# Seven block products in place of eight for the gate and up projections of layer 1

## The chip, the cores and the metric

The kernel runs on one core of a Trainium2 chip. The time is device microseconds (us) of one execution. In a span lie the instructions of five engines that run beside each other: TensorE (PE: matmuls; PEld: its weight loads), VectorE (DVE), ScalarE (ACT), GpSimd (POOL) and SyncE (SP, which here only issues DMAs). Each engine takes its instructions in the written order; semaphores make one wait for another. POOL also issues most DMAs.

## The reference, cut to what matters

640 tokens (512 latent, 128 context) of width 1024 pass through two layers. Each layer is feed-forward, mixer (layer 0 attention, layer 1 a long convolution named Hyena), feed-forward; so there are four feed-forwards, and the changed ones are the two of layer 1. One is

```
h = x * (1 + scale) + shift
g, u = split(h @ w1)            # w1: 1024 x 5632, so g and u: 640 x 2816
f = (silu(g) * u) @ w2          # w2: 2816 x 1024
x = layer_norm(ALPHA * x + 0.5 * gate * f)
```

`shift`, `scale` and `gate` come from `silu(cond) @ ada_w`, nine vectors of 1024 for each layer. The Hyena mixer needs the spectra of its filters, which depend on the weights alone.

## The kernel before, in words

Everything is held transposed: features on the 128 partitions, 640 tokens along the row, in two halves of 320. To keep accuracy each operand is split in a high part rounded to the multiplier's format (fp32r) and a low part, the remainder; one product then takes three matmuls: high by high, high by low, low by high.

The program runs in this order: spectra of the Hyena filters with the first modulation vectors (`spectra`), feed-forward 0 of layer 0, attention, feed-forward 1 of layer 0, feed-forward 0 of layer 1, Hyena, feed-forward 1 of layer 1. By the profile's times these begin at about 0, 169, 640, 940, 1417, 1888 and 2257 us.

- `ffn`: the 2816 hidden features are 22 chunks of 128 in four parts (`PARTS`, 6, 6, 6 and 4). For each chunk `ffn1` computes g and u (L561: 8 blocks of 128 inputs, 2 outputs, 3 matmuls, for each half: 96 matmuls of 320 columns), then ACT takes SiLU (L569), DVE multiplies (L571) and `split` makes the high part on ACT (L93) and the low part on DVE (L94). After each part the second product runs (`mm_cols`, L522): an output tile of 128 features and one half takes 18 matmuls, and `resid` (L503, DVE) adds it to x.
- Weights come in units. `w_dma` (L113, POOL) loads one, which gives the high part; `w_split` copies it negated on ACT (L125) and adds the raw weights to it by an accumulating DMA that POOL issues (L126), which leaves the low part. `w_get(i)` splits a unit ahead while fewer than `wmax` (3) are live. They share 8 buffers.
- `bg_step` makes one block of 128 values of a modulation vector beside the feed-forward: two DVE reductions (L255) over a 512 KB piece of `ada_w`, which POOL loaded two steps ahead into one of two buffers (L241). Before, the steps of layer 1's vectors lie in feed-forward 1 of layer 0 (60 places) and feed-forward 0 of layer 1.
- `spectra` is a software pipeline of rounds r. In a round PE generates filter block r+6 (`gen`) and transforms block r (`xform`, L1104); DVE multiplies with the decay (`decay`, L1019), combines (`comb`, L1070), makes low parts (`lo`, L1088) and takes the larger of two magnitudes (`total`, L1046); ACT makes high parts (`hi`, L1080, L1082), magnitudes (`mags`, L1029) and stores the transforms (`store`, L1119). Low parts of the second of two operands come by an accumulating DMA of 256 KB (L1087).

PSUM holds 8 tiles, taken in turn for every product.

Of the kernel before, what the change touches and what calls it, by code (L numbers as in the profile page):

```python
# [21 lines left out]
FF = 2816  # L22
NF = 22
PARTS = [(0, 6), (6, 12), (12, 18), (18, 22)]
ALPHA = 4.0 ** 0.25
EPS = 1e-5
TWO_PI = (6.28125, 0.0019340515136718750, 1.255665914356996e-06)
# [15 lines left out]
class Kernel:  # L43
# [492 lines left out]
    def group_steps(self, us, fn):  # L536
# [4 lines left out]
                out.append((u, (lambda w, u=u, half=half: fn(w, u, half)), half == 1))  # L541
        return out

    def ffn(self, l, f, u0):
        nc = self.nc
        u = u0
        i_ln = 0 if f == 0 else 2
        sums = {}

        def ffn1(c):  # L550
            def fn(w, u, half):
                self.flush(f"ln{half}")
                a, z = self.half[half]
                wh, wl = w
                g = self.ps(name="g")
                uu = self.ps(name="u")
                for k in range(KD):
                    xh, xl = self.h[k]
                    for o, c0 in ((g, 0), (uu, P)):
                        for q, (s, m) in enumerate(((wh, xh), (wh, xl), (wl, xh))):  # L560
                            nc.tensor.matmul(o[:, 0:z - a], s[:, k, c0:c0 + P], m[:, a:z],  # L561
                                             start=(k == 0 and q == 0), stop=(k == 7 and q == 2))
                    self.clk(6 * 0.136)
                ci = c - part[0]
                if ci not in acts:
                    acts[ci] = (self.b(dt=F32R, name="ah"), self.b(dt=F32R, name="al"))
                ah, al = acts[ci]
                sg = self.t((P, z - a), name="sg")
                nc.scalar.activation(out=sg, in_=g[:, 0:z - a], func=AF.Silu)  # L569
                ac = self.t((P, z - a), name="ac")  # L570
                nc.vector.tensor_tensor(out=ac, in0=sg, in1=uu[:, 0:z - a], op=ALU.mult)  # L571
                self.split(ah[:, a:z], al[:, a:z], ac)
            return fn

        for pi, part in enumerate(PARTS):
            acts = {}
            fin = pi == len(PARTS) - 1
            c = part[0]
            while c < part[1] - fin:
                n = 3 if c == 0 else 1  # L580
                self.run_steps(self.group_steps(range(u, u + n), lambda w, q, half, d=c - u: ffn1(q + d)(w, q, half)), c > 0)
                u += n
                c += n
            if pi == 0:
                self.flush("ln0x")
                self.flush("ln1x")
                gt = self.gate(l, 2 + 3 * (2 if f else 0), 0.5)
            ks = [(q, q) for q in range(part[1] - part[0])]
            if not fin:
                for jj in range(4):  # L590
                    w = self.w_get(u)
                    for j2 in range(2):
                        for half in range(2):
                            ps = self.ps(name="f")
                            self.mm_cols(ps, w, j2 * P, acts, ks, half)
                            self.resid(ps, jj * 2 + j2, half, gt)
                        self.bg_step()
                    self.w_done(u)
                    u += 1
            else:  # L600
                out = (l, f) == (1, 1)
                if out:
                    self.half, self.seg = HALF2, SEG2
                else:
                    GB = self.sh(l, i_ln)

                def fn(w, q, half, u=u, c=c):
                    if q == u:
                        ffn1(c)(w, q, half)
# [12 lines left out]
                self.run_steps(self.group_steps(range(u, u + 3), fn))  # L622
                u += 3
        return u
# [345 lines left out]
    def spectra(self):  # L970
# [18 lines left out]
        def w3_hi(n):  # L989
            w3[n] = [self.fp.tile([P, 512], F32R, tag="w3", name="w3", bufs=6) for _ in range(3)]  # L990
            nc.scalar.activation(out=w3[n][0], in_=self.xs(2), func=AF.Copy)
            nc.scalar.activation(out=w3[n][1], in_=self.xs(0), func=AF.Copy)

        def w3_lo(n):
            wa, wb, wl = w3[n]
            nc.vector.tensor_tensor(out=wl[0:64], in0=self.xs(2)[0:64], in1=wa[0:64].bitcast(F32), op=ALU.subtract)
            nc.vector.tensor_tensor(out=wl[64:P], in0=self.xs(0)[64:P], in1=wb[64:P].bitcast(F32), op=ALU.subtract)
            if n + 1 < 4:
                self.w3_load(n + 1)

# [131 lines left out]
        for r in range(-6, NI):  # L1132
# [4 lines left out]
            on(decay, r + 5)  # L1137

            ahead = [r + 2] if r < 14 else [16, 17] if r == 14 else [r + 3]
            middle = r % 5 == 1 and 0 <= r + 5 < NI  # L1140
            if middle:
                on(mags, r + 5)
                mid(r + 5)
            for i in ahead:
                on(comb, i)
                on(hi, i)
                on(lo, i)
            if not middle:
                on(mags, r + 5)
# [417 lines left out]
    def run(self):  # L1567
        nc, tc, I, O = self.nc, self.tc, self.I, self.O
        with ExitStack() as es:
# [36 lines left out]
            with tc.tile_pool(name="fq", bufs=1) as fq:  # L1606
                self.ada_pool(fq, 16 * KD)
                u = self.ffn(0, 1, u)
                u = self.ffn(1, 0, u)
                self.need_mods(1, range(9))  # L1610
            with tc.tile_pool(name="hp", bufs=1) as self.ap:
                u = self.hyena(u)
            u = self.ffn(1, 1, u)
            for h in range(2):
                self.flush(f"ln{h}")

    def add_ffn_units(self, units, l, f):
        I = self.I
        for pi, (p0, p1) in enumerate(PARTS):
            for c in range(p0, p1):  # L1620
                units.append((I["w1"][l, f, c], [P, KD, 256]))
# [8 lines left out]
def host_layout(i):  # L1630
# [148 lines left out]
```

## Time and profile before

| | us |
|---|---|
| median of 3 runs | 2754.49 (2753.18 to 2756.75) |
| profiled execution | 2754.99 |
| its span | 2753.2 |
| PE busy | 2657.8 (97%) |
| DVE, ACT, POOL busy | 1319.8, 890.2, 724.4 |
| mean granted TensorE clock | 0.988 of full |

Matmuls overlap, so their durations (about 310 ns) are longer than their distance. The distance comes from the chain of waits, where a run of matmuls stands as one piece. In a list of groups the last columns tell the busy time, the mean duration and the idle time of the engine before, with who ended it.

### The profile page before, as it was taken

The numbers are of one execution on the slowest core, as the hardware profiler recorded it, in microseconds if no ns is written. First come the engines' busy times: TensorE is split into PE (matmuls) and PEld (weight loads), VectorE is DVE, ScalarE is ACT, GpSimd is POOL, SyncE is SP. The second block draws the span as 40 slices with busy tenths as digits, with TensorE's granted clock in tenths as the row PEclk, the third lists the DMA queues.
The fourth block names the chain that finished last, engine by engine and source line by source line (L and its number), as shares of the span: only waits on it lengthen the run. The fifth ranks groups of instructions, "written<-read, shape, count | busy, mean of one in ns | idle before, by whom it ended". The sixth has DMA issues, their size and how long they took to land.

```text
span 2753.2 us, 42540 instructions
## 1 busy us (share of the span) xinstructions
PE 2657.8 (97%) x17402; PEld 2519.5 (92%) x17402; DVE 1319.8 (48%) x2894; ACT 890.2 (32%) x1518; POOL 724.4 (26%) x980
## 2 busy tenths in 40 slices
PE   8889999999899999999999999999999899999997
PEld 3679999998845899999999999999999899999997
DVE  6845555627864446555555311116439843211114
ACT  3662212125675332222242222124323333122222
POOL 3521121215122422121241111114119742101103
PEclk9999999999999999999999999999999999999998
DMA  7667978854302669797856856663653365656561
GB/s 244 195 194 200 283 216 242 233 156 106 95 16 61 169 155 254 202 264 208 256 131 178 215 141 154 145 165 95 181 168 130 109 180 131 164 129 176 129 163 54
DMA packets 91802, 460.22 MB, mean 167 GB/s; under 512 B 10975, under 2 KB 16687, under 8 KB 57560
## 3 DMA queue, kind: packets, MB, share of 16 engines
q0 software_dynamic: 71136, 405.50, 56.1%
q1 hardware_dynamic: 20104, 51.96, 5.5%
q8 instruction: 137, 2.24, 0.3%
q14 instruction: 57, 0.47, 0.1%
q10 hardware_dynamic: 368, 0.04, 0.0%
HBM read 436.22 MB, written 16.01 MB: 164 GB/s over the span
## 4 chain that ended last, share of the span: by engine, by line
PE 63%; issue 15%; DVE 6%; POOL 5%; DMA 2%; ACT 2%; SPq 0%; POOLq 0%; DVEq 0%; ACTq 0%
PE f L522 18%; PE g L561 17%; PE u L561 17%; PE u L522 6%; PE o L815 2%; POOL ar L241 1%; PE pt L804 1%; POOL wh L113 1%; DMA wl<-w 1%; DVE yl L1383 1%; DVE q L682 1%; POOL wl L126 1%; PE s L780 1%; DVE p L1354 1%; PE s L781 0%
## 5 line engine op out<-in xcount | busy, mean ns | idle before, releaser
L125 ACT ACTIVATE wl<-wh 128x2048 fp32r<-128x2048 f32 (+1 forms) x167 | 297.8, 1783 | 449.5 <-PE f L522 351.5
L561 PE MATMUL g<-hh,wl 128*128 128x320 f32 (+1 forms) x1408 | 435.8, 310 | 3.4 <-DMA wl<-w 3.4
L522 PE MATMUL f<-al,wh 128*128 128x320 f32 (+2 forms) x1408 | 436.5, 310 | 2.1 <-DVE al L94 1.6
L522 PE MATMUL f<-ah,wl 128*128 128x320 f32 (+2 forms) x1408 | 435.9, 310 | 1.7 <-DMA wl<-w2a 1.0
L522 PE MATMUL f<-ah,wh 128*128 128x320 f32 (+2 forms) x1408 | 437.3, 311 | 0.0
L561 PE MATMUL g<-hh,wh 128*128 128x320 f32 (+1 forms) x1408 | 437.3, 311 | 0.0
L561 PE MATMUL g<-hl,wh 128*128 128x320 f32 (+1 forms) x1408 | 435.7, 309 | 0.0
L561 PE MATMUL u<-hh,wl 128*128 128x320 f32 (+1 forms) x1408 | 435.5, 309 | 0.0
L561 PE MATMUL u<-hl,wh 128*128 128x320 f32 (+1 forms) x1408 | 435.5, 309 | 0.0
L561 PE MATMUL u<-hh,wh 128*128 128x320 f32 (+1 forms) x1408 | 435.5, 309 | 0.0
L571 DVE TENSOR_TENSOR ac<-sg,u 128x320 f32<-128x320 f32 (+1 forms) x176 | 85.8, 487 | 671.8 <-ACT sg L569 671.6
L503 DVE SCALAR_TENSOR_TENSOR x<-f,gate,x 128x128 f32<-128x128 f32 (+3 forms) x432 | 173.6, 435 | 314.7 <-PE f L522 314.2
L569 ACT ACTIVATE sg<-g 128x320 f32<-128x320 f32 (+1 forms) x176 | 76.9, 437 | 758.4 <-PE g L561 758.4
L522 PEld LDWEIGHTS f<-al,wh 128*128 128x128 f32 x1408 | 265.2, 188 | 3.9 <-DVE al L94 3.7
L561 PEld LDWEIGHTS g<-hh,wl 128*128 128x128 f32 x1408 | 264.7, 188 | 3.9 <-DMA wl<-w 3.9
L522 PEld LDWEIGHTS f<-ah,wl 128*128 128x128 f32 x1408 | 265.1, 188 | 2.2 <-DMA wl<-w2a 1.2
L522 PEld LDWEIGHTS f<-ah,wh 128*128 128x128 f32 x1408 | 265.1, 188 | 1.0 <-ACT ah L93 0.5
L561 PEld LDWEIGHTS g<-hl,wh 128*128 128x128 f32 x1408 | 264.6, 188 | 1.2 <-POOL hl L318 0.5
L561 PEld LDWEIGHTS g<-hh,wh 128*128 128x128 f32 x1408 | 264.7, 188 | 0.5
L561 PEld LDWEIGHTS u<-hl,wh 128*128 128x128 f32 x1408 | 264.8, 188 | 0.0
L561 PEld LDWEIGHTS u<-hh,wh 128*128 128x128 f32 x1408 | 264.7, 188 | 0.0
L561 PEld LDWEIGHTS u<-hh,wl 128*128 128x128 f32 x1408 | 264.7, 188 | 0.0
(315 smaller groups left out, 4685.5 us busy)
## 6 DMA issues: line engine op xcount, KB each, us to landing
wh<-w POOLq DMA_DIRECT2D x86, 1024.0 KB, 11.2
wl<-w POOLq DMA_DIRECT2D x86, 1024.0 KB, 9.1
ar<-ada_w POOLq DMA_DIRECT2D x128, 512.0 KB, 5.9
wh<-w2a POOLq DMA_DIRECT2D x48, 768.0 KB, 10.7
wl<-w2a POOLq DMA_DIRECT2D x48, 768.0 KB, 9.2
wh<-hyin POOLq DMA_DIRECT2D x12, 1024.0 KB, 10.8
wl<-hyin POOLq DMA_DIRECT2D x12, 1024.0 KB, 8.0
wr<-ada_first SPq DMA_DIRECT2D x8, 1024.0 KB
```

The source lines that it names most:

```text
L113: nc.gpsimd.dma_start(out=r, in_=src)
L125: self.nc.scalar.activation(out=lo, in_=hi.bitcast(F32), func=AF.Copy, scale=-1.0)
L126: self.nc.gpsimd.dma_start(out=lo, in_=self.units[i][0], accum_op=ALU.add)
L241: self.nc.gpsimd.dma_start(out=self.ada_raw[n], in_=self.I["ada_w"][l, m, j])
L503: nc.vector.scalar_tensor_tensor(out=self.x[:, j, s0:s1], in0=ps[:, s0 - a:s1 - a], scalar=gate[:, tk, j:j + 1], in1=self.x[:, j, s0:s1], ...
L522: nc.tensor.matmul(ps[:, 0:z - a], s[:, kw, c0:c0 + P], m[:, a:z], start=(first and i == 0 and q == 0), stop=(last and i == n - 1 and q == 2))
L561: nc.tensor.matmul(o[:, 0:z - a], s[:, k, c0:c0 + P], m[:, a:z], start=(k == 0 and q == 0), stop=(k == 7 and q == 2))
L569: nc.scalar.activation(out=sg, in_=g[:, 0:z - a], func=AF.Silu)
L571: nc.vector.tensor_tensor(out=ac, in0=sg, in1=uu[:, 0:z - a], op=ALU.mult)
L682: nc.vector.tensor_tensor(out=tiles[r][R[1 - r], c], in0=x[R[r]], in1=tiles[r][R[r], c].bitcast(F32), op=ALU.subtract)
L780: nc.tensor.matmul(ps[:, 0:n], x, kh[t][:, r, c0:c0 + n], start=True, stop=False)
L815: nc.tensor.matmul(ob[R[r], :], v[:, vs[c], g * 64:(g + 1) * 64], pts.pop((b, g, c)), start=(c == 0), stop=(c == len(vs) - 1))
```

## The change

1. Layer 1's feed-forwards take `ffn_s`. Chunks 0, 1, 2 and 21 are computed as before. For chunks 3 to 20 `s_unit` treats inputs in two halves (r), tokens in two halves of 320 and outputs as gate and up, and computes the 2x2 block product with seven products instead of eight (Winograd's form of Strassen's scheme). A product is 4 blocks of 128 inputs by 3 matmuls of 320 columns, 12 matmuls; a chunk is 84.
2. The sums of token blocks are made once for each feed-forward (`s_tokens`: POOL adds high and low parts again, DVE makes four sums, `split` parts them). The sums of weight blocks are made for every chunk one chunk ahead (`s_weights`, four pieces p0 to p3, called from `hooks` between the products): SP loads four blocks of 256 KB, POOL makes two sums, DVE two more, ACT and DVE split them, and the three plain blocks get their low part by an accumulating DMA.
3. The hidden features are seven parts of 3, 3, 3, 3, 3, 3 and 4 chunks (`PARTS7`). In the second product a tile takes 9 matmuls.
4. All modulation vectors of layer 1 are made in feed-forward 1 of layer 0: in the second products of its first two parts `bg_step` runs twice at each place (76 places for 72 steps).
5. In `spectra` magnitudes and their sum are of block r+4 and no longer r+5, so they follow the decay by a round; the low part of the filters' last weights comes by two accumulating DMAs after the first group.

```diff
+    def s_weights(self, c, nxt):
...
+        def block(n, g, r):
+            h, l = ops[n]
+            x = A.pop((c, g, r)) if n == "a22" else A[c, g, r]
+            nc.scalar.activation(out=h, in_=x, func=AF.Copy)
+            nc.scalar.activation(out=l, in_=x, func=AF.Copy, scale=-1.0)
+            nc.gpsimd.dma_start(out=l, in_=self.I["w1s"][self.sf, c, g, r], accum_op=ALU.add)
+
+        def p0():
...
+            block("a11", 0, 0)
+            nc.gpsimd.tensor_tensor(out=st["s"][:, 1], in0=A[c, 1, 0], in1=A[c, 1, 1], op=ALU.add)
+            block("a12", 0, 1)
...
+        def p1():
+            slot(("s2", "s3"))
+            nc.vector.tensor_tensor(out=st["d"], in0=st["s"][:, 1], in1=A[c, 0, 0], op=ALU.subtract)
+            nc.gpsimd.tensor_tensor(out=st["s"][:, 0], in0=A.pop((c, 0, 0)), in1=A.pop((c, 1, 0)), op=ALU.subtract)
+            self.split(*ops["s2"], st["d"])
+            self.split(*ops["s3"], st["s"][:, 0])
...
+        def p2():
+            slot(("a22", "s1"))
+            block("a22", 1, 1)
+            nc.vector.tensor_tensor(out=st["d"], in0=A.pop((c, 0, 1)), in1=st["d"], op=ALU.subtract)
+            self.split(*ops["s1"], st["s"][:, 1])
...
+        def p3():
+            slot(("s4",))
+            self.split(*ops["s4"], st["d"])
...
+    def s_unit(self, c, acts, ci, hooks):
...
+        x = prod("a11", B[0, 0])
+        nc.scalar.activation(out=s1, in_=x, func=AF.Copy)
+        hook(0)
+        x = prod("a12", B[1, 0])
+        add(sg, s1, x)
+        nc.scalar.activation(out=sg, in_=sg, func=AF.Silu)
+        hook(1)
+        x = prod("s2", Tn[2])
+        add(u2, s1, x)
+        hook(2)
+        x = prod("s3", Tn[3])
+        add(u3, u2, x)
+        hook(3)
+        x = prod("a22", Tn[4])
+        add(s1, u3, x)
+        nc.vector.tensor_tensor(out=s1, in0=sg, in1=s1, op=ALU.mult)
+        self.split(ah[:, n], al[:, n], s1)
+        hook(4)
+        x = prod("s1", Tn[1])
+        add(u2, u2, x)
+        add(u3, u3, x)
+        hook(5)
+        x = prod("s4", B[1, 1])
+        add(u2, u2, x)
+        nc.scalar.activation(out=u2, in_=u2, func=AF.Silu)
+        nc.vector.tensor_tensor(out=u3, in0=u2, in1=u3, op=ALU.mult)
+        self.split(ah[:, 320:T], al[:, 320:T], u3)
...
+                if i < 2:
+                    w = self.s_weights(c + 1, after[c + 1])
+                    hooks = {0: w[0], 1: w[1], 3: w[2], 5: w[3]}
+                if i == 1:
+                    def cast(m=u + 1):
+                        self.wlim = m
+                        self.w_dma(m)
+                    hooks[4] = cast
+                if i == 2:
+                    def cast(m=u + 2):
...
+                    hooks[0] = cast
+                    hooks[2] = self.w_split
+                self.s_unit(c, acts, i, hooks)
+            if not fin:
+                w = self.s_weights(c1, after[c1])
+                second(u, acts, gt, {1: w[0], 4: w[1], 7: w[2], 10: w[3]})
...
                         self.bg_step()
+                        if pi < 2 and f:
+                            self.bg_step()
...
-            if not middle:
-                on(mags, r + 5)
-            on(total, r + 5)
+            on(total, r + 4)
```

On ACT, in a feed-forward of layer 1, two halves of a chunk read before as SiLU (`sg`), high part of the activations (`ah`), and then the copy of a unit's weights (`wl`):

```order
L569 ACTIVATE sg_14891<-g_14839 128x320
L93 ACTIVATE ah_14889<-ac_14893 128x320
L569 ACTIVATE sg_14947<-g_14897 128x320
L93 ACTIVATE ah_14889<-ac_14949 128x320
L125 ACTIVATE wl_14953<-wh_14718 128x1536
```

Now it reads as below in the second chunk of a part and the beginning of the third. `sw` are the operands of the next chunk, made from the raw blocks `sr` or the sums `s13` and `s24`; `sa` are the activations, `sm` a product, `wl` the low part of the second product's first weights.

```order
L95 ACTIVATE sw_14296<-s13_14269 128x512
L619 ACTIVATE sw_14333<-sr_14192 128x512
L620 ACTIVATE sw_14333<-sr_14192 128x512
L95 ACTIVATE sw_14333<-s13_14269 128x512
L95 ACTIVATE sa_14253<-s1_14249 128x320
L95 ACTIVATE sw_14378<-s24_14270 128x512
L708 ACTIVATE u2_14250<-u2_14250 128x320
L95 ACTIVATE sa_14253<-u3_14251 128x320
L685 ACTIVATE s1_14399<-sm_14405 128x320
L689 ACTIVATE sg_14402<-sg_14402 128x320
L127 ACTIVATE wl_14450<-wh_14361 128x1536
```

The third chunk's first product (L685) stands behind the last activation of the second (L95 `sa`), and `wl` behind the third chunk's first SiLU.

On POOL, in feed-forward 1 of layer 0, the second product of the first part read before with two pieces of `ada_w` (`ar`) for each unit of weights:

```order
L126 DMA wl<-w2a 128x1536
L113 DMA wh<-w 128x2048
L241 DMA ar<-ada_w 128x1024 x2
L126 DMA wl<-w 128x2048
L113 DMA wh<-w 128x2048
```

and now, at the same place, with four:

```order
L128 DMA wl<-w2a 128x1536
L115 DMA wh<-w 128x2048
L243 DMA ar<-ada_w 128x1024 x4
L128 DMA wl<-w 128x2048
L115 DMA wh<-w 128x2048
```

A unit's accumulating DMA (`wl`) stands behind twice as many pieces, each of which waits for a step of DVE.

On ACT in `spectra`, a round read before with the high parts (`sh`, `sl`) ahead of the magnitudes (`am`) and the stores (`sg`):

```order
L1080 ACTIVATE sh<-cb 128x512 x2
L1082 ACTIVATE sl<-cb 128x512
L1029 ACTIVATE am<-ab 128x512 x2
L1119 ACTIVATE sg<-xf 128x2x256 x2
L1080 ACTIVATE sh<-cb 128x512 x2
```

Now the magnitudes stand first, and they are of the block whose decay was in the round before:

```order
L1281 ACTIVATE am<-ab 128x512 x2
L1332 ACTIVATE sh<-cb 128x512 x2
L1334 ACTIVATE sl<-cb 128x512
L1371 ACTIVATE sg<-xf 128x2x256 x2
L1281 ACTIVATE am<-ab 128x512 x2
```

In a round they have moved from behind `sl` to the front.

## Rows read from the trace of the kernel before

**Rows 1.** The page: busy time of each engine, its share, instructions.
```profile
PE 2657.8 (97%) x17402; PEld 2519.5 (92%) x17402; DVE 1319.8 (48%) x2894; ACT 890.2 (32%) x1518; POOL 724.4 (26%) x980
```
**Rows 2.** Windows: the engines' busy us (instructions), PE clock, DMA share, GB/s.
```profile
50.00:150.00 100.00, 82.80 (x333) 60.59 (x331) 78.41 (x108) 67.97 (x126) 53.46 (x54) 0.93 0.63 174
...
1033.00:1075.00 42.00, 42.00 (x288) 42.00 (x287) 28.21 (x55) 7.24 (x6) 9.58 (x15) 1.00 0.89 256
...
1547.00:1631.00 84.00, 84.00 (x575) 84.00 (x574) 11.46 (x24) 20.09 (x28) 8.53 (x12) 1.00 0.57 144
...
2347.00:2389.00 42.00, 42.00 (x289) 42.00 (x288) 10.20 (x25) 7.57 (x6) 5.69 (x8) 1.00 0.70 169
```
**Rows 3.** Chain of waits, 1550 to 1700 us: start, length, engine, line, matmuls.
```profile
1549.87 0.44 PE g L561 x3
...
1631.71 42.24 PE f L522 x288
```
**Rows 4.** Groups by line in feed-forwards: busy us, mean ns, idle before, who ended it.
```profile
L571 DVE TENSOR_TENSOR ac<-sg,u 128x320 f32<-128x320 f32 x174 | 84.8, 487 | 659.7 <-ACT sg L569 659.6
L94 DVE TENSOR_TENSOR al<-ac,ah 128x320 fp32r<-128x320 f32 x174 | 87.0, 500 | 93.6 <-ACT ah L93 93.6
L93 ACT ACTIVATE ah<-ac 128x320 fp32r<-128x320 f32 x174 | 82.1, 472 | 114.2 <-DVE ac L571 114.2
L569 ACT ACTIVATE sg<-g 128x320 f32<-128x320 f32 x174 | 76.0, 437 | 732.1 <-PE g L561 732.1
L125 ACT ACTIVATE wl<-wh 128x1536 fp32r<-128x1536 f32 x48 | 70.8, 1475 | 96.3 <-PE f L522 56.3 <-issue 40.0
L503 DVE SCALAR_TENSOR_TENSOR x<-f,gate,x 128x320 f32<-128x320 f32 x136 | 74.7, 549 | 154.6 <-PE f L522 154.3
```
**Rows 5.** Timeline of DVE, ACT and POOL, two stretches of `spectra`: start, length, what.
```profile
77.74 1.28 DVE L1070 TENSOR_TENSOR cb<-ab 128x512 f32<-128x512 f32 x2
79.12 0.69 DVE L1088 TENSOR_TENSOR sl<-cb,sh 128x512 fp32r<-128x512 f32 x1
81.28 0.69 DVE L1046 TENSOR_TENSOR am<-am 128x512 f32<-128x512 f32 x1 [1.47 <-ACT am L1029]
...
80.12 1.13 ACT L1029 ACTIVATE am<-ab 128x512 f32<-128x512 f32 x2
...
49.89 1.27 POOL L1050 TENSOR_TENSOR am<-am 128x512 f32<-128x512 f32 x1 [0.68 <-DVE am L1046]
51.12 1.71 POOL L1023 TENSOR_TENSOR ab<-ab 1x512 f32<-1x512 f32 x1
...
50.85 2.53 DVE L1070 TENSOR_TENSOR cb<-ab 128x512 f32<-128x512 f32 x2
```
**Rows 6.** Timeline of POOL, 1555 to 1610 us.
```profile
1606.34 0.87 POOL L126 DMA_DIRECT2D wl<-w2a  x1 [12.23 <-ACT wl L125]
1606.90 0.86 POOL L113 DMA_DIRECT2D wh<-w2a  x1
```
**Rows 7.** Landing times: issues of L126 at 1600 to 1780, 1560 to 1605 us; the page.
```profile
DMA to landing us min/median/max: 6.6/7.8/8.4
...
DMA to landing us min/median/max: 7.9/7.9/7.9
...
sl<-cb POOLq DMA_DIRECT2D x16, 256.0 KB, 3.3
```
**Rows 8.** Timeline of DVE, 1048 to 1076 us, and landing of `ada_w` pieces there.
```profile
1054.33 1.13 DVE L503 SCALAR_TENSOR_TENSOR x<-f,gate,x 128x320 f32<-128x320 f32 x3
1055.38 1.28 DVE L255 CUSTOM_DVE_ANT_0 prod<-ar,cond,ab 128x1024 f32<-128x1024 f32 x1
...
1057.91 0.55 DVE L503 SCALAR_TENSOR_TENSOR x<-f,gate,x 128x320 f32<-128x320 f32 x1
...
DMA to landing us min/median/max: 4.3/6.1/9.8
```
**Rows 9.** Waits from 0 to 172 us: who waited for whom, total, times, longest.
```profile
DVE am L1046 <- ACT am L1029: 24.2, 16, 4.7
PE xf L1104 <- ACT sg L1119: 13.5, 6, 5.0
```

More of the change, by code (lines that the diff above doesn't have):

```diff
@@ L542, in group_steps, with act_pair, ffn1, fn @@
         return out
+    def act_pair(self):
+        return self.b(dt=F32R, name="ah"), self.b(dt=F32R, name="al")
+    def ffn1(self, acts, ci, new):
+        nc = self.nc
+        def fn(w, u, half):
+            self.flush(f"ln{half}")
+            a, z = self.half[half]
+            wh, wl = w
+            g = self.ps(name="g")
+            uu = self.ps(name="u")
+            for k in range(KD):
+                xh, xl = self.h[k]
+                for o, c0 in ((g, 0), (uu, P)):
+                    for q, (s, m) in enumerate(((wh, xh), (wh, xl), (wl, xh))):
+                        nc.tensor.matmul(o[:, 0:z - a], s[:, k, c0:c0 + P], m[:, a:z],
+                                         start=(k == 0 and q == 0), stop=(k == 7 and q == 2))
+                self.clk(6 * 0.136)
+            if ci not in acts:
+                acts[ci] = new()
+            ah, al = acts[ci]
+            sg = self.t((P, z - a), name="sg")
+            nc.scalar.activation(out=sg, in_=g[:, 0:z - a], func=AF.Silu)
+            ac = self.t((P, z - a), name="ac")
+            nc.vector.tensor_tensor(out=ac, in0=sg, in1=uu[:, 0:z - a], op=ALU.mult)
+            self.split(ah[:, a:z], al[:, a:z], ac)
+        return fn
@@ new lines, in s_tokens @@
+    def s_tokens(self, k):
+        nc = self.nc
+        B = {}
+        for r in range(2):
+            hh, hl = self.h[k + 4 * r]
+            for c in range(2):
+                cs = slice(320 * c, 320 * c + 320)
+                B[r, c] = self.t((P, 320), name="sb")
+                nc.gpsimd.tensor_tensor(out=B[r, c], in0=hh[:, cs].bitcast(F32), in1=hl[:, cs].bitcast(F32), op=ALU.add)
+        t1, t3, t2, t4 = B[0, 0], B[0, 1], B[1, 1], B[1, 0]
+        nc.vector.tensor_tensor(out=t1, in0=t3, in1=t1, op=ALU.subtract)
+        nc.vector.tensor_tensor(out=t3, in0=t2, in1=t3, op=ALU.subtract)
+        nc.vector.tensor_tensor(out=t2, in0=t2, in1=t1, op=ALU.subtract)
+        nc.vector.tensor_tensor(out=t4, in0=t4, in1=t2, op=ALU.subtract)
+        for n, t in ((2, t2), (3, t3), (1, t1), (4, t4)):
+            o = self.b((P, 2, 320), F32R, name="st")
+            self.split(o[:, 0], o[:, 1], t)
+            self.st[n, k] = (o[:, 0], o[:, 1])
@@ new lines, in s_unit, with prod, hook, add @@
+    def s_unit(self, c, acts, ci, hooks):
+        nc = self.nc
+        ops = self.sops.pop(c)
+        B = {(r, j): [tuple(x[:, 320 * j:320 * j + 320] for x in self.h[k + 4 * r]) for k in range(4)] for r, j in ((0, 0), (1, 0), (1, 1))}
+        Tn = {n: [self.st[n, k] for k in range(4)] for n in (1, 2, 3, 4)}
+        def prod(name, m):
+            ps = self.ps(name="sm")
+            wh, wl = ops[name]
+            for k in range(4):
+                mh, ml = m[k]
+                for q, (s, x) in enumerate(((wh, mh), (wh, ml), (wl, mh))):
+                    nc.tensor.matmul(ps[:, 0:320], s[:, k], x, start=(k == 0 and q == 0), stop=(k == 3 and q == 2))
+                self.clk(3 * 0.136)
+            return ps[:, 0:320]
+        def hook(i):
+            if hooks.get(i):
+                hooks[i]()
+        def add(o, a, b):
+            nc.vector.tensor_tensor(out=o, in0=a, in1=b, op=ALU.add)
+        n = slice(0, 320)
+        s1, u2, u3, sg = (self.t((P, 320), name=q) for q in ("s1", "u2", "u3", "sg"))
+        acts[ci] = tuple(self.sp.tile([P, T], F32R, tag="sa", name="sa", bufs=6) for _ in range(2)) if ci < 3 else self.act_pair()
+        ah, al = acts[ci]
+        x = prod("a11", B[0, 0])
[25 more added lines that the diff above has]
+        self.split(ah[:, 320:T], al[:, 320:T], u3)
+        hook(6)
@@ L550, in ffn1 @@
         def ffn1(c):
[L551 to L573, printed above, removed]
+            return self.ffn1(acts, c - part[0], self.act_pair)
         for pi, part in enumerate(PARTS):
```

135 lines of the change are left out of this document (125 added, 10 removed).

## The prediction

> **What bounds the kernel now.** I read the page first: PE is busy for 97% of the span [rows 1], the others for half or less. Since matmuls overlap, busy time alone would not prove a bound, so the next view was the windows by stage: in both kinds of feed-forward stretch PE has no idle time and the full clock, 84.00 of 84.00 us and 42.00 of 42.00, while DVE is at 11.46 and 10.20 us, ACT and POOL lower still except for ACT's 20.09 [rows 2]. Then the chain of waits: from 1550 to 1700 us it is matmuls and nothing else, 3 in 0.44 us and 288 in 42.24 us, so one matmul of 320 columns takes 42.24 / 288 = 0.1467 us of the path [rows 3]. Whatever takes matmuls out of a feed-forward shortens the span by that much each, as long as nothing else becomes late. Only `spectra` at the start is different: from 50 to 150 us PE is busy 82.80 of 100 us, at 0.93 of the clock, DVE 78.41 [rows 2], and the longest of DVE's waits is for ACT's magnitudes, 24.2 us in 16 waits [rows 9].
>
> **Matmuls removed.** A chunk had 96 matmuls and has 84. Chunks 3 to 20 in two feed-forwards are 36. 36 x 12 x 0.1467 = **-63.4 us**. The second product keeps its count; its 3 extra parts add 3 x 24 evictions in each feed-forward, 144 in all, of at most 0.549 us on DVE [rows 4]. A tile of 9 matmuls lasts 1.32 us on PE and its eviction half of that, and DVE was idle for 32 of 42 us there [rows 2]: nothing.
>
> **The chain inside a chunk.** A product is 12 matmuls, 1.76 us, a chunk 12.32 us of PE. The other engines must now do more in that time, and in order. From the rows: a 128x512 DVE operation comes every 0.60 us and ends after 0.68 (two in 1.28), one of ACT 0.52 and 0.61 (two in 1.13), a POOL addition of that size takes 1.27 [rows 5]; POOL goes on 0.56 us after issuing a DMA [rows 6]; 128x320 operations end after 0.44 to 0.50 us [rows 4] and I let them follow each other every 0.40 on DVE, 0.36 on ACT (scaled from the wider ones). Walk from the start of the first chunk of a part, all engines free. Product 0 is out at 1.92 us; ACT copies it and makes both parts of a11, till 3.44. POOL issues the accumulating DMA and only then adds the two raw blocks: 5.35. DVE's difference: 6.08. ACT's high part: 6.73. DVE's low parts of s2 and s3 wait for POOL's second addition: 7.8 and 8.6. Then u2, u3: 9.5; the second difference and the low part of s1: 10.7; gate times up and its split: 12.7; two additions, the low part of s4 and the last addition: 14.5; SiLU, product, ACT's copy: 16.05. ACT takes the next chunk's first product at 15.94 instead of 1.95 + 12.32 = 14.27. So the **chain takes 14.0 us where PE takes 12.3**, and the chunks that prepare operands (two of three) fall behind by 1.67 us each, 3.3 us by the third. PSUM hides this: the lag is two products of eight. Operands of the next chunk are ready too: the last wait is a12's DMA, issued at 5.3 to 6.1, 3.3 us to land [rows 7], before 12.3.
>
> What it does not hide is the second product's first weights. Their copy stands behind the third chunk's first SiLU, which is late with the chain: the addition for it waits for DVE's last work on the chunk before, 30.6 us after the part's start, SiLU ends at 31.5, the copy of 1.475 us [rows 4] at 32.9, and the accumulating DMA of 768 KB takes 6.6 us to land [rows 7]: 39.6. PE wants it as its third matmul after 3 x 12.32 us: 37.26. PE waits **2.3 us** in each of 5 parts. In the sixth part the unit is 1 MB, 0.43 us more on ACT (scaled) and 7.9 us to land [rows 7]: 41.3, a wait of 4.05. Two feed-forwards: 2 x (5 x 2.3 + 4.05) = **+31 us**. The second unit is not late: its copy ends at 40.6, it lands at 47.2, wanted near 50. Bounds: if the chain keeps up with PE, the landing is at 37.4 and the sum is about +5; if the chain takes 16.5 us (below), each wait is 5 us longer, +91. I take the walk's value.
>
> Beside POOL's work DVE's own can stretch: two combinations of 1.28 us took 2.53 when POOL's 1.71 us operation ran over them [rows 5], while those beside nothing took 1.28. The Trainium skill says why (SBUF — State Buffer, section SBUF: two separate sides): GpSimd and a DVE operation with two SBUF inputs share one pair of ports, whoever comes first keeps it for the whole instruction. This case's rows agree: the stretch, 1.25 us, is most of POOL's operation. The walk has one such wait; the rival below takes all.
>
> **Raw blocks, token sums, wait for buffers.** SP's 4 loads a chunk, 1 MB, and 3 accumulations, 0.75 MB, come to less than the 2 MB a chunk took before at a DMA share of 0.57 [rows 2]: nothing. The token sums lie beside the first three chunks, where PE needs 42 us: nothing. Weight tiles are taken in an order in which the eighth last is always read already: nothing. If one of these came late, PE would wait once in a feed-forward for some us.
>
> **Steps moved into layer 0.** In the second product of the first two parts of feed-forward 1, one place is two tiles, 36 matmuls, 5.28 us. DVE's evictions there take 1.05 us and a step 2.53 [rows 8]: 3.6 us, now 6.1, 0.8 over. Moreover the step's buffer is loaded again only after it, in 6.1 us (4.3 to 9.8) [rows 8], so a round cannot be shorter than 2.5 + 6.1 = 8.6 us. Over 8 places the lag is 8 x 0.8 = 6.6 us at the least and 8 x 3.3 = 27 with the median. Eight PSUM tiles cover 7 x 2.64 = 18.5 us. The DMA share there is 0.89 at 256 GB/s [rows 2]; 8 more pieces of 0.5 MB in 42 us are 98 GB/s more, too much for that stretch, so weights come late too. Per part 0 to 8.5 us, twice: 0 to 17 us; in the ffn1 stretch behind it the lag is made up. I take half, **+8 us**. Afterwards layer 1 has no steps: nothing, DVE was hidden there.
>
> **Spectra.** With the magnitudes a round earlier in ACT's order DVE's wait for them goes, 24.2 us in 16 waits, 1.47 us typical [rows 5, 9]; the low part of the filters moves off DVE as well. What is late next is PE itself, 82.80 of 100 us [rows 2]: at most 17 us can go there, and 13.5 us of PE's waits are for ACT's stores [rows 9], which come sooner. The last 20 us hang on ACT and DVE splitting the first weights and stay. I take **-16 us**, between 0 (the gain is lost in the tail) and -24.
>
> **Sum.** The profiled execution, 2754.99 us: span 2753.2 and 1.8 around it; that is 0.5 over the median. 2755.0 - 63.4 + 31 + 8 - 16 = 2714.6, less that 0.5: **2714 us**, 1.5% faster.
>
> **Rivals.**
> - *The chain keeps up* (DVE and ACT run tighter than my walk, or wait less for POOL): PE's waits in layer 1 are about +5. 2755.0 - 63.4 + 5 + 4 - 16 = 2684. For it: DVE's plain work in a chunk is only 11 operations of 0.40 and 6 of 0.60, 8 us of 12.3. Against it: POOL stands in the middle, behind a DMA issue.
> - *The gains beside the matmuls don't come*: spectra 0, steps in layer 0 +17, waits as walked: 2755 - 63 + 31 + 17 = 2740. For it: the DMA share of 0.89. Against it: the 24 us of DVE's waits go for certain.
> - *The chain becomes the bound; slower.* Every two-input operation of DVE that meets one of POOL's two additions waits it out: 2 x 1.25 us a chunk, a chain of 16.5 us. The wait for the first weights then is 2.3 + 2 x 2.5 = 7.3 us in 10 parts and 9 in two: +91 us; 2755.0 - 63.4 + 91 + 8 - 16 = 2775. It turns at a chain of 15.7 us, where the waits, 24 x (15.7 - 14.0) + 31 = 72, eat the other terms. For it: the stretch of 1.25 us is in the trace. Against it: most of DVE's work there reads one operand from PSUM, and such operations keep their 0.68 us beside POOL.
> - *The change does not do what it says*: PE's time for a product would have to be over 1.76 us. Sizes, types and order of a matmul are those of before, so I give it no chance of its own.
>
> **Chances and range.** Forecast (own range 2696 to 2731) 0.50; the chain keeps up 0.25; gains missing 0.15; chain bound 0.10. Range 2678 to 2750, which leaves out the slower case and the best of the second. A difference under 0.2%, 5.5 us, could not be told from none. Faster: 0.50 + 0.25 + 0.12 = 0.87; same 0.04; slower 0.09.
>
> **What would show it.** In the profile after: 12 matmuls of a product in 1.76 us of the chain; DMA low parts of the second product (`wl<-w2c`) as what ends PE's idle time, 10 times some 2 us, and `wl<-w` twice some 4; DVE busy for over 8 us of each chunk of 12.3; the wait of `total` for `mags` gone, and the first matmul of feed-forward 0 at about 153 us instead of 169; in feed-forward 1 of layer 0 PE idle at the end of the first two second products. I am wrong if PE's idle time lies at products within a chunk (operands late, or PSUM full), or at the first chunk of layer 1.

## The result, and the profile after

The changed kernel takes 2895.24 us (median of 4, 2891.27 to 2896.11) against 2754.98 us for the kernel before (median of 4): a ratio of 1.0508, interval 1.0496 to 1.0521. It is 5.1% slower where 1.5% faster was forecast, and far outside the range. Taken from the first matmul of one stage to the first of the next, in the profiled executions, the stages last (us):

| stage | before | after | difference | forecast |
|---|---|---|---|---|
| spectra | 169.5 | 167.0 | -2.5 | -16 |
| feed-forward 0 of layer 0, attention | 770.9 | 769.6 | -1.3 | 0 |
| feed-forward 1 of layer 0 | 477.1 | 528.5 | +51.4 | +8 |
| feed-forward 0 of layer 1, to Hyena's long matmuls | 491.6 | 535.7 | +44.1 | -16 |
| Hyena | 350.8 | 353.5 | +2.7 | 0 |
| feed-forward 1 of layer 1, to the end | 493.3 | 538.8 | +45.5 | -16 |
| span | 2753.2 | 2893.1 | +139.9 | -40.4 |

The first line of the profile's page, to be read beside [rows 1], shows that PE has 432 matmuls less, but is busy for 92% of the span instead of 97%.

```profile
PE 2648.9 (92%) x16970; PEld 2505.6 (87%) x16970; DVE 1709.7 (59%) x3564; ACT 1043.8 (36%) x1916; POOL 887.7 (31%) x1126
```

The windows by stage of the changed kernel, columns as in [rows 2]. First the spectra, then a second product and the first products behind it in feed-forward 1 of layer 0, then in feed-forward 0 of layer 1 three chunks of seven products, and pieces of the second product behind them (the last two rows look closer at the end of its wait):

```profile
50.00:150.00 100.00, 81.81 (x335) 62.98 (x334) 77.69 (x103) 73.97 (x135) 51.02 (x56) 0.90 0.72 194
1029.00:1073.00 44.00, 42.85 (x292) 42.44 (x290) 29.59 (x55) 7.43 (x6) 8.60 (x15) 1.00 0.65 197
1073.00:1182.00 109.00, 90.48 (x576) 89.84 (x576) 61.51 (x107) 19.83 (x29) 20.77 (x34) 0.91 0.82 230
1544.00:1581.00 37.00, 36.92 (x252) 36.66 (x250) 26.21 (x48) 15.74 (x32) 11.58 (x12) 1.00 0.65 158
1581.00:1588.00 7.00, 0.53 (x2) 0.30 (x2) 2.92 (x7) 4.49 (x6) 0.92 (x2) 0.84 0.49 93
...
1586.00:1590.00 4.00, 0.39 (x1) 0.39 (x2) 0.49 (x1) 3.74 (x6) 1.88 (x3) 0.50 0.99 171
1590.00:1594.00 4.00, 4.00 (x21) 4.00 (x21) 0.97 (x2) 0.00 (x0) 3.30 (x3) 0.68 0.89 174
```

The three chunks are what was meant: 252 matmuls in 37 us, PE full. In the 109 us lie 576 matmuls, which take 576 x 0.1467 = 84.5 us without a gap. PE's waits (who waited for whom, total, times, longest) over feed-forward 0 of layer 1, then over feed-forward 1 of layer 0, which had 3.0 us of waiting for `wl<-w` before:

```profile
PE f L524 <- DMA wl<-w2c: 32.1, 5, 7.9
PE g L563 <- DMA wl<-w: 9.2, 1, 9.2
PE f L524 <- DVE sa L96: 5.1, 1, 5.1
PE f L524 <- DMA wl<-w2b: 3.4, 1, 3.4
...
PE g L563 <- DMA wl<-w: 40.3, 7, 10.0
```

So the rows that were to show the waits are there (`wl<-w2c`, `wl<-w`), two to three times as long as walked (6.4 us on the mean and 9.2, instead of 2.3 and 4.05), and the stretch that was to make up the steps' lag is where it is paid. Inside the chunks PE waits too, for low parts of the operands that come by DMA, 5.6 us in the whole span (of a list of groups, columns as in [rows 4]):

```profile
L669 PE MATMUL sm<-st,sw 128*128 128x320 f32 x1728 | 261.4, 309 | 5.6 <-DMA sw<-w1s 5.6
```

**Inside a chunk.** The timeline of ACT, POOL and DVE in the second part (start, length, operation, idle time before). L685 is ACT's copy of a chunk's first product, so the distance from one L685 to the next is the length of the chain:

```profile
1613.82 0.44 ACT L685 ACTIVATE s<-sm 128x320 f32<-128x320 f32 x1 [9.84 <-PE sm L669]
1616.16 1.63 POOL L628 TENSOR_TENSOR s<-sr 128x512 f32<-128x512 f32 x1
1617.82 2.70 DVE L635 TENSOR_TENSOR s<-s,sr 128x512 f32<-128x512 f32 x1 [1.69 <-POOL s L628]
1618.01 1.96 POOL L636 TENSOR_TENSOR s<-sr 128x512 f32<-128x512 f32 x1
1620.56 1.15 ACT L95 ACTIVATE sw<-s 128x512 fp32r<-128x512 f32 x2 [3.87 <-DVE s L635]
...
1629.90 0.42 ACT L685 ACTIVATE s<-sm 128x320 f32<-128x320 f32 x1
1646.01 0.42 ACT L685 ACTIVATE s<-sm 128x320 f32<-128x320 f32 x1
```

The chain is 16.1 us, not 14.0. DVE's first difference (L635) takes 2.70 us here and ends 0.55 us after POOL's second sum (L636). In 24 of its 36 times it meets that sum, takes 1.97 to 2.71 us and ends 0.56 after it; in the 12 others, made beside a second product, the sum is long over, and it takes 0.68. ACT waits 3.87 us for it, and all that stands behind ACT's split shifts.

**Steps.** Shown are DVE's reductions that belong to the second product of the first part of feed-forward 1 of layer 0 (the first of each step; PE is already at the first products behind it), then the DMAs that POOL issues:

```profile
1086.29 1.28 DVE L257 CUSTOM_DVE_ANT_0 prod<-ar,cond,ab 128x1024 f32<-128x1024 f32 x1 [6.95 <-DMA ar<-ada_w]
1088.83 1.28 DVE L257 CUSTOM_DVE_ANT_0 prod<-ar,cond,ab 128x1024 f32<-128x1024 f32 x1
1092.90 1.28 DVE L257 CUSTOM_DVE_ANT_0 prod<-ar,cond,ab 128x1024 f32<-128x1024 f32 x1 [0.41 <-DMA ar<-ada_w]
1095.99 1.28 DVE L257 CUSTOM_DVE_ANT_0 prod<-ar,cond,ab 128x1024 f32<-128x1024 f32 x1 [0.47 <-DMA ar<-ada_w]
1107.52 1.28 DVE L257 CUSTOM_DVE_ANT_0 prod<-ar,cond,ab 128x1024 f32<-128x1024 f32 x1 [7.86 <-DMA ar<-ada_w]
...
1089.21 0.53 POOL L243 DMA_DIRECT2D ar<-ada_w  x1 [9.85 <-DVE mods L257]
1092.04 0.53 POOL L243 DMA_DIRECT2D ar<-ada_w  x1 [2.31 <-DVE x L505]
1092.56 0.92 POOL L128 DMA_DIRECT2D wl<-w  x1
1093.11 0.92 POOL L115 DMA_DIRECT2D wh<-w  x1
```

The landing times of the pieces issued at 1089 to 1092.5 us, then of those at 1095 to 1099 us:

```profile
DMA to landing us min/median/max: 3.7/3.8/3.9
...
DMA to landing us min/median/max: 9.8/10.8/11.7
```

Four steps and one unit of weights go round in 21.2 us (1086.29 to 1107.52), while PE uses up a unit of the second product in 72 x 0.1467 = 10.6 us. Two pieces land in 3.8 us; the two issued behind the unit's 2 MB land in 9.8 to 11.7, and DVE stands still for 7 to 8 us. The next unit's DMAs are behind the steps on POOL, so weights come once in a round. PSUM covers the second product itself; the loss comes in the first products of the next part.

### The profile page after: what moved, and what is told of

Read it like the earlier page. It is cut to its first block, busy times and chain, and to the rows that moved or that the text cites. A ratio compares the mean times of both kernels' runs of the same rounds, so it can differ in the third digit from the quotient of the medians.

```text
span 2893.1 us, 43816 instructions
## 1 busy us (share of the span) xinstructions
PE 2648.9 (92%) x16970; PEld 2505.6 (87%) x16970; DVE 1709.7 (59%) x3564; ACT 1043.8 (36%) x1916; POOL 887.7 (31%) x1126
## 4 chain that ended last, share of the span: by engine, by line
PE 51%; issue 21%; DVE 11%; DMA 7%; POOL 6%; ACT 4%; SPq 0%; POOLq 0%; DVEq 0%; ACTq 0%
PE f L524 18%; PE g L563 8%; PE u L563 8%; PE u L524 5%; PE sm L669 4%; DMA wl<-w2c 2%; PE o L1061 2%; PE pt L1050 1%; DMA wl<-w 1%; DVE s L635 1%; POOL ar L243 1%; POOL wh L115 1%; PE adar L211 1%; POOL s L628 1%; POOL sw L621 1%
## 5 line engine op out<-in xcount | busy, mean ns | idle before, releaser
L505 DVE SCALAR_TENSOR_TENSOR x<-f,gate,x 128x192 f32<-128x192 f32 (+2 forms) x576 | 227.1, 435 | 277.0 <-PE f L524 276.4
L524 PE MATMUL f<-sa,wh 128*128 128x320 f32 (+2 forms) x1344 | 321.9, 328 | 15.9 <-DVE sa L96 9.7
L524 PE MATMUL f<-sa,wl 128*128 128x320 f32 (+2 forms) x672 | 222.6, 331 | 69.8 <-DMA wl<-w2c 63.0
L669 PE MATMUL sm<-st,sw 128*128 128x320 f32 x1728 | 261.4, 309 | 5.6 <-DMA sw<-w1s 5.6
L524 PEld LDWEIGHTS f<-sa,wh 128*128 128x128 f32 x1344 | 247.0, 206 | 18.0 <-DVE sa L96 10.2
L669 PEld LDWEIGHTS sm<-st,sw 128*128 128x128 f32 x1728 | 254.9, 188 | 7.7 <-DMA sw<-w1s 7.7
L563 PE MATMUL g<-hl,wh 128*128 128x320 f32 (+1 forms) x832 | 260.2, 313 | 0.0
L524 PE MATMUL f<-ah,wl 128*128 128x320 f32 (+2 forms) x736 | 228.1, 310 | 2.7 <-DMA wl<-w2a 2.7
L524 PE MATMUL f<-al,wh 128*128 128x320 f32 (+2 forms) x736 | 228.6, 311 | 2.1 <-DVE al L96 1.6
L524 PE MATMUL f<-ah,wh 128*128 128x320 f32 (+2 forms) x736 | 229.0, 311 | 0.0
```

The lines of the kernel that those rows point to most:

```text
L505: nc.vector.scalar_tensor_tensor(out=self.x[:, j, s0:s1], in0=ps[:, s0 - a:s1 - a], scalar=gate[:, tk, j:j + 1], in1=self.x[:, j, s0:s1], ...
L524: nc.tensor.matmul(ps[:, 0:z - a], s[:, kw, c0:c0 + P], m[:, a:z], start=(first and i == 0 and q == 0), stop=(last and i == n - 1 and q == 2))
L669: nc.tensor.matmul(ps[:, 0:320], s[:, k], x, start=(k == 0 and q == 0), stop=(k == 3 and q == 2))
```

## The experiments

Six theories are tested:

- **A**: the shared port. POOL's sum holds up DVE's difference, and that makes the chain long.
- **B**: POOL is simply late.
- **C**: the weights are late by the order of their copies and DMAs.
- **D**: the loads of `ada_w` pieces go round in two buffers, and the weights stand behind them.
- **E**: the stage has too many bytes to load.
- **F**: DVE's own work stands ahead of its evictions of PSUM.

The times are medians of 4 to 10; each run stands beside runs of the kernel before on the same chip.

**One sum of weights on DVE.**

```
-            nc.gpsimd.tensor_tensor(out=st["s"][:, 0], ..., op=ALU.subtract)
+            nc.vector.tensor_tensor(out=st["s"][:, 0], ..., op=ALU.subtract)
```

> The changed kernel (2895 us) with one operation a chunk moved: the second sum of raw weight blocks (L636) is made by DVE, no longer by POOL. Theory A (shared port): DVE's difference L635, which takes 2.70 us beside POOL's sum and 0.68 alone, is stretched by it, and that is what makes the chain of a chunk 16.1 us long. Then L635 takes 0.7 to 1.0 us, the chain falls to about 16.1 - 2.0 + 0.6 = 14.7 us, each of the 10 waits of PE for the first weights of a second product is some 2.8 us shorter and about 1 us of lost clock goes with it: 2895 - 10 x 3.8 = about 2857 us. Rival B (POOL is simply late: its DMA issues and its first sum set the chain): L635 still starts as late and the chain stays above 15.5 us: 2880 us or more.

2835.9 us, ratio 1.0301 (1.0278 to 1.0324): 59 us less than the changed kernel, more than A's 38. DVE, and ACT's copies, in the second part of this run:

```profile
1605.89 0.69 DVE L635 TENSOR_TENSOR s<-s,sr 128x512 f32<-128x512 f32 x1 [1.68 <-POOL s L628]
1606.50 0.69 DVE L636 TENSOR_TENSOR s<-sr 128x512 f32<-128x512 f32 x1
...
1601.89 0.44 ACT L685 ACTIVATE s<-sm 128x320 f32<-128x320 f32 x1 [9.83 <-PE sm L669]
1615.96 0.42 ACT L685 ACTIVATE s<-sm 128x320 f32<-128x320 f32 x1
1630.06 0.42 ACT L685 ACTIVATE s<-sm 128x320 f32<-128x320 f32 x1
```

The window of the second product ahead of it:

```profile
1574.20:1600.10 25.90, 23.03 (x147) 22.78 (x147) 14.45 (x32) 7.74 (x13) 4.72 (x5) 0.93 0.59 123
```

L635 is back at 0.69 us though it still waits for POOL's first sum, and the chain is 14.1 us. That is A, not B. The gain is above A's because the chain falls by 2.0 us and not by 1.4. It is now as long as the one that the prediction walked, and PE waits 25.90 - 23.03 = 2.9 us, near the walked 2.3; but the second product is 25.9 - 147 x 0.1467 = 4.3 us longer than its matmuls. The other 1.4 us go with the granted clock, 0.93 of full over it.

**Both sums of weights on DVE** (L628 as well).

> The changed kernel with both sums of raw weight blocks (L628, L636) on DVE; POOL only issues DMAs beside the chunks. Theories A and B both expect a chain no longer than PE's 12.3 us: the third chunk's SiLU comes 7 us earlier and PE's wait for the second product's first weights falls from 6 to 8 us to 0 to 1: 2895 - 10 x 8.5 = about 2810 us. Rival C (the weights are late by the order of their copy and their DMA, whatever the chain does): waits of 4 us or more stay, 2850 us or more. The waits in the first second product (5.08 us for activations beside the token sums) stay in all three.

2799.52 us, ratio 1.0166 (1.0146 to 1.0186), 96 us less than the changed kernel. The second part's chunks before a second product, and that product:

```profile
1540.00:1577.00 37.00, 37.00 (x255) 37.00 (x253) 27.06 (x57) 18.27 (x35) 7.16 (x9) 1.00 0.74 185
1576.80:1598.80 22.00, 21.58 (x147) 21.32 (x146) 14.96 (x33) 7.76 (x13) 3.44 (x4) 1.00 0.54 120
```

The chain keeps up (ACT's copies are 12.1 to 12.9 us apart) and the wait is 0.4 us here. C is refuted for the five parts; it is not for the last part, where waits of 2.1, 1.1 and 5.3 us stay. In the first second product PE still waits 5.1 us, for DVE's `sa` and not for weights.

**Steps spread over the first products, one more for each chunk.**

```
-                        if pi < 2 and f:
-                            self.bg_step()
...
             if bg:
                 self.bg_step()
+            if bg > 1 and last:
+                self.bg_step()
```

> The changed kernel, with the second steps of modulation vectors taken out of the second products of feed-forward 1 of layer 0 and put into its first products, one after the second half of each chunk (15 places for 12 steps). Theory D (round trip: with two buffers a place with two steps lasts until both pieces are loaded again, and the weights of the next unit are issued behind them): the stage falls from 528.5 us to about 478 us, the time to about 2845 us. Rival E (there are simply too many bytes in the stage): the same bytes are still loaded in the same stage, which stays above 500 us; 2870 us or more.

2871.05 us, ratio 1.0422 (1.0401 to 1.0444): 24 us less, half of what D had said, and what E had expected (2870 or more, the stage above 500). The stage is 510.5 us. D itself is not refuted: three steps and a unit of weights (2 MB) now stand in one round, which takes 17 to 19 us where PE has 14.1 for a chunk; of the pieces issued at 1098 to 1152 us the median landed after 8.3 us, the last after 11.4. The expectation took a spread load for a load that fits. This run alone did not tell D from E; the next did.

**Four buffers for the pieces, steps doubled as in the change.**

```
-            self.ada_raw[n] = self.adp.tile([P, D], F32, tag="ar", name="ar", bufs=2)
+            self.ada_raw[n] = self.adp.tile([P, D], F32, tag="ar", name="ar", bufs=self.ada_b)
-        self.ada_load(n + 2)
+        self.ada_load(n + self.ada_b)
```

> The changed kernel with four buffers for the pieces of ada_w in feed-forward 1 of layer 0 (each loaded four steps ahead), where there were two. Steps stay doubled. Theory D (round trip of two buffers): a place then waits for pieces issued a place earlier, 10 us, that land in 4 to 11: most of the 51 us goes, 2850 to 2865 us. Rival E (bytes: 2 MB of weights and 2 MB of pieces for 10.6 us of PE in a second product): the time stays at 2880 us or more.

2844.22 us, ratio 1.0324 (1.0305 to 1.0344): 51 us less. The second product of the first part and the first products behind it:

```profile
1027.00:1070.00 43.00, 43.00 (x295) 43.00 (x294) 39.79 (x72) 7.62 (x6) 10.74 (x18) 1.00 0.88 265
1070.00:1155.00 85.00, 85.00 (x582) 85.00 (x581) 50.49 (x90) 20.22 (x29) 18.65 (x30) 1.00 0.90 267
```

The same bytes are loaded in the same stage, at 265 GB/s, and PE has no gap: E is refuted, D is shown. The queues had been idle in part for lack of buffers (a DMA share of 0.65 in the changed kernel), not full.

**The doubled steps alone, in the kernel before.**

> The kernel before (2755 us) with one part of the change alone: two steps at each place in the second products of the first two parts of feed-forward 1 of layer 0. Theory D: the 51 us that this stage is longer in the changed kernel come from this edit alone: 2755 + 51 = about 2805 us, and nothing comes back in feed-forward 0 of layer 1, which has no steps left. The prediction's own sum had +8: 2763 us. A rival that blames the stage's loss on anything else of the changed kernel expects under 2770 us.

2805.43 us, ratio 1.0191 (1.0176 to 1.0207), as D expected to the microsecond. The first products behind the first doubled second product:

```profile
1077.00:1185.00 108.00, 90.49 (x577) 89.70 (x576) 62.28 (x109) 19.64 (x28) 22.04 (x36) 0.91 0.82 229
```

This is nearly the changed kernel's row (109 us, 90.48 busy, 0.91). Feed-forward 0 of layer 1, freed of its steps, lasts 491.5 us instead of 491.6: nothing comes back.

**The spectra's edits alone, in the kernel before.**

> The kernel before with only the edits in the spectra. If the 2.5 us by which feed-forward 0 starts earlier in the changed kernel are what the edits give, 2752 us; if the 16 us of the prediction were there and something else of the changed kernel hid them, 2739 us.

2750.62 us, ratio 0.9991 (0.9982 to 1.0001): 2.7 us, not told from none by its interval. In the changed kernel's spectra the wait of `total` for `mags` is all but gone, as forecast, and others stand in its place (from 0 to 168 us, beside [rows 9]):

```profile
POOL sl L1339 <- DVE am L1298: 29.3, 11, 6.9
DVE sl L1340 <- ACT sh L1332: 17.0, 6, 4.9
DVE am L1298 <- ACT am L1281: 1.0, 1, 1.0
```

DVE hardly waits with `total` any more, but with the low part behind it (4.9 us in all before); POOL's accumulating DMAs, which waited 29.2 us for ACT's `sl` before, wait 29.3 us for DVE's `am`. PE is busy 81.81 of 100 us, no more than before [rows 2].

**Sums of weights and of tokens on DVE, four buffers.**

```
-                nc.gpsimd.tensor_tensor(out=B[r, c], in0=hh[:, cs]..., op=ALU.add)
+                nc.vector.tensor_tensor(out=B[r, c], in0=hh[:, cs]..., op=ALU.add)
```

The token sums were moved for what the changed kernel shows ahead of its first second product; DVE and POOL there:

```profile
1515.74 5.92 DVE L96 TENSOR_TENSOR sa<-ac,sa 128x320 fp32r<-128x320 f32 x1 [0.54 <-ACT sa L95]
1515.27 6.03 POOL L586 TENSOR_TENSOR sb<-hh,hl 128x320 f32<-128x320 f32 x7
```

A subtraction of 0.49 us lasts as long as seven sums of POOL, and PE waits 5.1 us for its result.

> The changed kernel with three mends: both sums of weight blocks on DVE, the sums of token blocks on DVE too, and four buffers for the pieces of ada_w. Theories A and D together, with causes that do not touch each other: 2895 - 96 - 51, and the token sums: a subtraction that takes 5.92 us beside POOL's sums takes 0.49, the first second product of each feed-forward loses 11 us less: 2 x 9 = 18. About 2730 us, some 25 us faster than the kernel before. If the token sums are late for another reason, 2748 us.

2744.99 us, ratio 0.9964 (0.9952 to 0.9975): the two mends add up (2895 - 96 - 51 = 2748), and the kernel is now 0.4% faster than the one before. But the token sums give 3 us, not 18. With them on DVE no operation is stretched there, and the first second product still takes 30.1 us.

**Weights for the second product earlier**, on top of the run above.

```
                     def cast(m=u + 2):
-                        self.wlim = m
+                        self.wlim = m + fin
                         self.w_dma(m)
+                        self.w_split()
                     hooks[0] = cast
-                    hooks[2] = self.w_split
+                    if fin:
+                        hooks[4] = self.w_split
```

> The same three mends, and the copies for the second product's first weights one place earlier (ahead of the third chunk's SiLU); in the last part the second unit is also copied in the third chunk and the third unit loaded there. In the run with the weight sums on DVE PE still waits 0.4 to 1.8 us before each second product and 2.1, 1.1 and 5 us in the last part. If those waits are the order of the copies, they go: with the clock that each takes, 10 x 1 + 2 x 12 = 34 us less than the run with three mends, about 2696 us. If they are DMA time that no order hides, no more than 10 us go.

2720.82 us, ratio 0.9884 (0.9867 to 0.99): 24 us less than the run above, between the two expectations and nearer the first. The windows show the first second product, a later one, and the last part's tiles (14.9 us, 24 in the run with the weight sums on DVE):

```profile
1457.60:1487.70 30.10, 25.10 (x147) 24.33 (x146) 28.00 (x67) 12.34 (x25) 3.49 (x4) 0.89 0.37 73
1584.20:1605.70 21.50, 21.50 (x148) 21.35 (x147) 14.86 (x33) 7.75 (x13) 3.47 (x4) 1.00 0.55 123
1828.90:1843.80 14.90, 14.65 (x100) 14.38 (x99) 4.84 (x9) 0.75 (x2) 5.22 (x6) 1.00 0.68 207
```

DVE in the first second product:

```profile
1468.06 2.94 DVE L394 TENSOR_SCALAR x<-x,lnga,lnba 128x320 f32<-128x320 f32 x8
1471.19 1.01 DVE L506 SCALAR_TENSOR_TENSOR x<-f,gate,x 128x320 f32<-128x320 f32 x2
```

Most of the gain is in the last part, as C has it there. What is left in the first second product: DVE is busy 28.00 of 30.10 us, and its first eviction comes 13.6 us after the start, when all 8 tiles of PSUM (8 x 1.32 us) are full.

**Token sums later.**

```
-            if n > 2:
+            if 2 < n < 5:
                 self.s_tokens(n - 3)
...
-        second(u + 3, acts, gt, {1: lambda: self.s_tokens(3), 6: ...
+        second(u + 3, acts, gt, {1: lambda: self.s_tokens(2), 4: lambda: self.s_tokens(3), 6: ...
```

> The run with the weights earlier (2721 us), with the sums of the third and fourth pair of token blocks taken from ahead of the first second product's first evictions to its second and fifth tile. There DVE worked without a gap from 1445 to 1490 us, the first eviction came at 1471.2 us, 13.6 us after the product's start, and PE lost 9 us with its 8 PSUM tiles full. Theory F (DVE's own work stands ahead of the evictions): the first eviction comes 5 us earlier, and PE loses 4 to 5 us less in each of two feed-forwards, though the sums are only put off: about 2712 us. Rival: DVE's total work there is the limit, not its order: no change within 3 us.

2717.87 us, ratio 0.9863 (0.9847 to 0.988), the fastest version. The same product, and what PE waits for in it:

```profile
1458.00:1484.30 26.30, 21.87 (x147) 21.33 (x146) 24.20 (x59) 10.36 (x22) 2.62 (x3) 1.00 0.28 45
...
PE f L525 <- DVE x L506: 2.8, 1, 2.8
PE f L525 <- DMA wl<-w2c: 1.6, 1, 1.6
```

It is 3.8 us shorter, as F says of the place; but the time falls by only 3 us where F had 9. That is the rival's bound, and hardly more than the runs scatter (2718.66 to 2722.53, and 2712.09 to 2718.9). Part of the gain is lost in the three chunks behind the product, which take 37.8 us here and 37.4 in the second feed-forward instead of 37.0; where the rest goes is not shown. The wait of 2.8 us that is left is for an eviction behind the last round of token sums, which keep DVE from 1474.0 to 1479.3 us.

**The layer norm's last step on ACT.** The same with L393's `x * lnga + lnba` as an activation with scale and bias.

> As the run with the token sums later, and the 16 multiplications and additions of the layer norm ahead of each feed-forward of layer 1 (L393, 0.36 us each on DVE) on ACT, which is free there. Theory F: the first eviction again 2.9 us earlier and 5.7 us of DVE's work gone from the stretch: about 2705 us. If DVE's total work is the limit, this run alone gains, 6 us in each feed-forward.

2719.68 us, ratio 0.9871 (0.9856 to 0.9885): no change, and neither side was right. DVE's work went down, but ACT's SiLU now stood behind eight of the new operations (4.46 us) and DVE waited 5.45 us for it. Of the 5 us that the product still has over its matmuls, PE waits 1.9 for an eviction and 2.2 for weights in this run; an order of DVE's work that removes the first was not tried.

## Why the prediction was wrong

By terms, from the traces (us; the durations of the products are from the first matmul of one group to the first of the next):

| term | forecast | measured |
|---|---|---|
| 432 matmuls less | -63.4 | -63: 252 matmuls in 37.0 us |
| waits, ten second products | +23 | +86: 28.6 to 30.7 each, 21.1 without a wait |
| waits in the last parts | +8 | +34 |
| first second products, token sums | 0 | +24 |
| doubled steps | +8 | +51 |
| spectra | -16 | -2.5 |
| the rest: three chunks take up to 38.4 instead of 37.0 (+9 in all), Hyena | 0 | +11 |

- **The matmuls removed** came out as worked. The loss is all in what was put beside them.
- **The chain inside a chunk** is the step that failed first: "DVE's difference: 6.08" gives the difference its undisturbed 0.68 us; in the trace POOL's second addition starts 0.19 us behind it, and it takes 2.70. The row for it was there, two combinations in 2.53 us instead of 1.28 [rows 5]; the walk applied it to a later operation and not to the one that meets the addition. It cost 2.0 us a chunk. "Operands of the next chunk are ready too" fell with it: PE waits 5.6 us in all for them, and the three chunks take up to 38.4 us; with the second sum on DVE they take 37.0. The rival with a chain of 16.5 us had the mechanism and nearly the size (16.1 measured, by one wait of 2.0 us where it had two of 1.25), and got a chance of 0.10. Its price of 7.3 us a wait nearly holds too (32.1 / 5 = 6.4, 7.9 at most), and yet its 2775 us were 120 short, for the reasons below.
- **The clock.** No term had it. In the windows above PE is idle for most of 1581 to 1588 us; from 1586 to 1590 the granted clock is 0.50, the lower level, 1.2 GHz, and from 1590 to 1594 PE works without a gap at 0.68, the mean of a stretch that begins at the lower level and ends at the upper. A wait of 8 us made the second product 9.7 us longer, the 18.5 us of waiting behind the doubled steps made 24.5. The Trainium skill (TensorE: Matmul & The Clock Gate, Part 1: The HAM clock gate) has the lower level for an idle engine and the upper for a busy one; the trace agrees, with 0.50 at the end of the wait and 1.00 from 1594 us on.
- **Steps moved into layer 0.** "8 x 0.8 = 6.6 us at the least and 8 x 3.3 = 27 with the median" took one landing time for all pieces and counted a place by one step. Two of four pieces land behind 2 MB of weights (10 to 12 us), and the weights are issued behind the steps: a loop of 21 us a unit. "In the ffn1 stretch behind it the lag is made up" was the wrong way round; there it is paid, 25 us a part. The reason given, a DMA share too high, was wrong too: with four buffers the stretch takes 265 GB/s without a gap.
- **Token sums.** "The token sums lie beside the first three chunks, where PE needs 42 us: nothing" looked at PE's time and not at DVE's order. Beside POOL's sums one subtraction grew to 5.92 us; with the sums on DVE it has 28 us of work in 30, and the layer norm and two rounds of sums stand ahead of the first eviction.
- **The last part** got the price of one wait (4.05). It has three: for the unit of the last chunk and for two units of the second product, each copied only when the one before is used.
- **Spectra.** The wait named did go, and the value taken, nearly all of PE's 17 us idle, was wrong: DVE and POOL wait in other places now, and PE is idle as long as before. That PE's idle time hangs on the whole circle of DVE, ACT and POOL is read from these waits and not shown by a run. The bound of 0 was the right end.

The Trainium skill (SBUF — State Buffer, SBUF: two separate sides) says that DVE and GpSimd lock a common pair of ports for a whole instruction. The rows agree that one engine's operation keeps out the other's (2.70 us against 0.69 with POOL's sum gone). But "whoever comes first keeps it" does not fit the recorded starts: in 22 of the 24 meetings DVE's difference is recorded 0.2 us ahead of POOL's sum (1617.82 and 1618.01 in the lines above), and yet ends behind it. The rows also go further: DVE was kept out through seven additions of POOL in a row, and an operation with a single wide input was held up too. Of the layer norm's (L393, 0.44 us alone), ahead of the changed kernel's first second product, one takes as long as four additions of POOL:

```profile
1503.69 4.04 DVE L393 TENSOR_SCALAR x<-x,lnga,lnba 128x320 f32<-128x320 f32 x1
1503.91 3.62 POOL L586 TENSOR_TENSOR sb<-hh,hl 128x320 f32<-128x320 f32 x4
```

## What to carry to other kernels

Walk a chain of engines with every pair of operations that share a port laid out in time, not with one allowance for all; a sum given to a free POOL can cost the busy DVE three times what it takes on DVE (2.0 us against 0.69), and both sums were cheaper on DVE (96 us here). Work in the background that waits for its own loads needs as many buffers as the slowest landing asks for, above all where other loads are issued behind it in the same queue: two more buffers were worth 51 us. And where PE had no gaps, one of some microseconds can be dearer than its length, since the clock falls in it (8 us of waiting made 9.7).

## What the runs showed of the hardware that was not expected

- POOL's 128x320 additions, one after another for 6.03 us, let no DVE operation in: 5.92 us for one of 0.49. Against one 128x512 addition of POOL (1.96 us) DVE's took 2.70 instead of 0.68. POOL's own took 1.96 there, and 1.63 for the sum before it, beside which DVE was idle.
- The DMA queues carried 265 GB/s at a share of 0.88 beside PE at its full clock, in a stretch that had been thought full at 256.
- A 512 KB piece lands in 3.7 to 3.9 us when issued ahead of a unit's 2 MB and in 9.8 to 11.7 behind them.
